# Hybrid pooling and HGRN2 decoder trunk: rectangles of the recurrence from packed key blocks, and the first weights behind the first rows

## The chip, the cores and the metric

One Trainium2 chip, one of its cores. The metric is the device time of one execution in microseconds (us). Three executions of the kernel before took 1765.79 to 1770.45 us, with a median of 1767.56.

## The reference

The input is 1024 tokens of 1024 channels, with 16 learned tokens put in front. There are two layers, each with a residual add: a pooling mixer, then a gated linear recurrence (HGRN2) of 16 heads of 128. All is float32.

```python
def _hgrn_chunk_step(S, xs):
    """One chunk of S_t = diag(f_t) S_{t-1} + k_t i_t^T, o_t = S_t^T q_t."""
    q, k, v, g = xs
    causal = jnp.tril(jnp.ones((c, c), dtype=bool))
    bcum = jnp.cumsum(g, axis=2)
    rel = bcum[:, :, :, None, :] - bcum[:, :, None, :, :]
    decay = jnp.exp(jnp.where(causal[:, :, None], rel, -jnp.inf))
    scores = jnp.einsum('bhtk,bhsk,bhtsk->bhts', q, k, decay)
    o = jnp.einsum('bhts,bhsv->bhtv', scores, v) + jnp.einsum('bhtk,bhkv->bhtv', q * jnp.exp(bcum), S)
    ...
def reference(x, meta_tokens, norm_w, ...):
    h = jnp.concatenate([meta, x], axis=1)
    for i in range(DEPTH):
        hn = rmsnorm(h, norm_w[i])
        y = pool_mixer(hn, ...) if i % N_MIXERS == 0 else hgrn2_mixer(hn, ...)
        h = h + y
    return rmsnorm(h[:, N_META:], final_norm_w)
```

The two big input projections are `h @ w_in` in both mixers; in the recurrence `w_in` gives q, f, i and gate.

## The kernel before

**Products.** The 1040 tokens are two passes of 520, each two halves of 260. A pair of blocks of a projection is made by seven products per pair of weight columns (`products`, names P1, P2, P6, P5, P7, P3, P4), each of 12 matmuls a pass (L413 to L415): the high and low part of the tokens (Th, Tl) with the high and low part of a weight (w). Both parts are made by ACT (a cast, L148) and DVE (a subtraction, L149). A product of both passes is 24 matmuls.

**Order of the work.** After each product `tick` moves a clock on by one and runs what is due. The pieces of a head's recurrence are put on that clock by `later` with the numbers of the table `PIECES`, so they lie between the products of the next head: `to32` at 8, `l32` at 9, `l64` at 10, `turn_k` at 11. Weights are made up to three products ahead (`LOOK`, `fill`). The framework that builds the program may still move an instruction on its engine's queue; each engine runs its own queue in order.

**The recurrence.** A head has Q and K as 128 channels by 1024 tokens, eight chunks of 128 tokens. `score` makes the part of the masked score matrix A inside blocks of 32 tokens from 4 products of a chunk each, 128 columns (L711). `to32` then scales Q and K by the decay of blocks of 32 (L716, L717). A level of block size h (`rect`, called by `level` for `l32` and `l64`) gives the rectangles of A where an odd block of h queries meets the even block of keys ahead of it:

```python
for c in range(NT):
    pe.matmul(b[:, c], lhsT=K0[:, c * P : (c + 1) * P], rhs=q4[:, c, 1::2], start=True, stop=True)
```

There are eight products (L664), one for a chunk, each with all 128 keys of the chunk as weights and its 64 odd queries as columns; half of what comes out isn't used. ACT copies the used blocks to A (L667), and `advance` scales odd Q and even K by the next decay (L655, L656) for the next level. `turn_k` transposes K for the states. A product of float32 operands stands in the profile as two records.

**Buffers.** A pool of 38 SBUF tiles of 128x1040 (`unit`) holds the tokens' parts, Q, K, F and what a head needs for a while.

**The start.** `load_tokens` loads the rows of the first pass in five tiles (16, 128, 128, 128 and 120 rows; `ht`). `first(i)` squares and sums a tile (L348 on ACT), makes rstd (L105 on DVE, L106 on POOL) and scales the rows (L353); `second(i)`, two steps behind, transposes them on PE (L366) and puts them into hn (L371 on ACT, L374 on DVE). `make_T` then builds the T tiles of the seven products from hn (L288). `ensure` loads the raw weights; for the first two raw buffers a copy of rstd is written into the buffer first (L185), so their loads can't be issued ahead of the tile that rstd is of:

```python
if i == 1:
    stat[0] = r
```

Of the kernel before, what the change touches and what calls it, by code (L numbers as in the profile page):

```python
# [14 lines left out]
P = 128  # L15
# [26 lines left out]
    "run": 0, "turn_v": 1, "inv0": 1, "inv1": 2, "scale_q": 2, "inv2": 3, "inv3": 4, "scale_k": 5, "scale_e": 6,  # L42
    "score0": 6, "score1": 7, "to32": 8, "l32": 9, "l64": 10, "turn_k": 11, "states": 12, "outs": 14, "normed": 16, "gated": 17,
}
# [7 lines left out]
def kernel(  # L52
# [38 lines left out]
    def atbank():  # L91
        return ps_at.tile([P, 512], F32, tag="at", name="at")
# [62 lines left out]
    def whole(fast):  # L155
# [171 lines left out]
        def tokens(p, w, ys=None, hts=None, lag=2):  # L327
# [3 lines left out]
            def first(i):  # L331
# [17 lines left out]
                rstd_into(r, ssq, tn, 1, D)  # L349
                if i == 1:  # L350
                    stat[0] = r
# [235 lines left out]
        def mixer1(steps):  # L587
# [61 lines left out]
            def advance(Q, K, h, fcur, fnext):  # L649

                nq, nk = Q.shape[1] // (2 * h), K.shape[1] // (2 * h)
                qe, qo = blocks(Q, h)
                ke, ko = blocks(K, h)
                fe, fo = blocks(fcur, 1)
                vec.tensor_tensor(qo, qo, fe[:, fe.shape[1] - nq :].broadcast_to([P, nq, h]), mul)  # L655
                vec.tensor_tensor(ke, ke, fo[:, fo.shape[1] - nk :].broadcast_to([P, nk, h]), mul)  # L656
                vec.tensor_tensor(fnext, fe[:, :, 0], fo[:, :, 0], mul)

            def rect(Q, K0, h):

                b = atbank().rearrange("p (c i) -> p c i", i=64)
                q4 = Q.rearrange("p (c b i) -> p c b i", c=NT, i=h)
                for c in range(NT):
                    pe.matmul(b[:, c], lhsT=K0[:, c * P : (c + 1) * P], rhs=q4[:, c, 1::2], start=True, stop=True)  # L664
                A3 = A.rearrange("p (c t) -> p c t", t=P)
                for i, s0 in enumerate(range(0, P, 2 * h)):
                    act.copy(A3[s0 : s0 + h, :, s0 + h : s0 + 2 * h], b[s0 : s0 + h, :, i * h : (i + 1) * h])  # L667

            def level(Q, K0, h, fcur, fnext):
                rect(Q, K0, h)  # L670
                advance(Q, K0, h, fcur, fnext)

            def intra_fast(Q, K, F, Fe):
# [40 lines left out]
                def to32():  # L714
                    q32, k32 = (a.rearrange("p (b i) -> p b i", i=32) for a in (Q, K0))
                    vec.tensor_tensor(q32, q32, ee.broadcast_to([P, 32, 32]), mul)  # L716
                    vec.tensor_tensor(k32, k32, eo.broadcast_to([P, 32, 32]), mul)  # L717
                    vec.tensor_tensor(Fe[:, 24:56], ee[:, :, 0], eo[:, :, 0], mul)
# [51 lines left out]
            def scan(n, Q, K, F, ti):  # L770
# [6 lines left out]
                def turn_v():  # L777
                    V = tl["V"] = unit("V")[:, :SEQ].rearrange("p (c v) -> p c v", v=P)
                    Vm = tl["Vm"] = cst.tile([P, P], F32, tag="Vm", name="Vm", bufs=2)
                    for b0 in (0, 4, 8):  # L780
# [5 lines left out]
                        if b0 < 8:  # L786
                            act.copy(V[:, b0 : b0 + 4], b)
                        else:
                            pool.memset(Vm, 0.0)
                            act.copy(Vm[:META], b[:META, 0])  # L790

                def turn_k():
# [60 lines left out]
                def gated():  # L853
# [14 lines left out]
                    "turn_v": turn_v, "turn_k": turn_k, "states": states, "outs": outs, "normed": normed, "gated": gated,  # L868
                    "l32": lambda: level(Q, K0, 32, Fe[:, 24:56], Fe[:, 0:16]),
                    "l64": lambda: level(Q, K0, 64, Fe[:, 0:16], dec),  # L870
                }
# [146 lines left out]
        for i, fn in enumerate(tokens(0, nw[0], hts=hts[0])):  # L1018
            fn()
            if i == 1:  # L1020
                ensure(1)
                hts.append([load_tokens(1, i) for i in range(len(TP[1]))])
            if i == len(TP[0]):
                fill()
# [59 lines left out]
```

## Time and profile before

| | us |
|---|---|
| median of three runs (lowest, highest) | 1767.56 (1765.79, 1770.45) |
| the profiled execution, its own time | 1768.34 |
| its span | 1766.6 |
| PE busy | 1696.1 |
| DVE busy | 1239.5 |
| ACT busy | 786.3 |

The span is what the profiler saw of the core's work; the execution's own time has the little around it too. Busy times are of instructions: PE's matmuls are pipelined, so the records overlap, and what a group of them takes on PE is read from the chain of work or from where the next ones start, not from their durations. An engine that is idle costs time only where the chain passes through its wait.

### The profile page before, as it was taken

Reading aid. Unit: us, or ns where it says so; the run is one execution under the profiler, and the core shown is the slowest. Engines: PE = TensorE matmul, PEld = TensorE weight load, DVE = VectorE, ACT = ScalarE, POOL = GpSimd, SP = SyncE. Lnnn points to the kernel's source line nnn. Section 1 sums busy time; section 2 is a strip of 40 time slices with the busy share of each in tenths; the row PEclk is TensorE's granted clock in tenths of the full one; section 3 lists DMA queues with packets and bytes.
Section 4 is the critical chain, followed back from the end, with each engine's and each line's share of the span. In section 5 each row is a group of like instructions: output and inputs, shape, how many; then the busy total and the mean of one; then the engine's idle time right before and its main releaser. Section 6 shows DMA issues by size and latency. Waiting matters only on the chain.

```text
span 1766.6 us, 32378 instructions
## 1 busy us (share of the span) xinstructions
PE 1696.1 (96%) x13315; PEld 1647.8 (93%) x13315; DVE 1239.5 (70%) x1959; ACT 786.3 (45%) x1746; POOL 55.2 (3%) x102
## 2 busy tenths in 40 slices
PE   3899999999998998799999999999999999999997
PEld 3799999999998998699999999999999999988886
DVE  5866677788237725898887787887887887884332
ACT  4533333345236525645554554544555545554221
POOL 1100000000000000000000000000000000000000
PEclk9799999999999999899999999999999999999999
DMA  4133233358337333222222212222212212254330
GB/s 133 37 127 102 97 97 109 109 188 282 96 113 261 104 112 115 66 77 69 79 62 66 84 61 72 67 65 75 84 49 78 67 61 85 76 175 143 113 107 33
DMA packets 191426, 176.56 MB, mean 100 GB/s; under 512 B 7093, under 2 KB 164485, under 8 KB 191269
## 3 DMA queue, kind: packets, MB, share of 16 engines
q1 hardware_dynamic: 191269, 174.40, 31.0%
q8 instruction: 107, 1.75, 0.4%
q14 instruction: 50, 0.41, 0.1%
HBM read 132.55 MB, written 41.81 MB: 99 GB/s over the span
## 4 chain that ended last, share of the span: by engine, by line
PE 88%; DVE 6%; ACT 2%; DMA 2%; issue 1%; SPq 0%; POOL 0%; DVEq 0%; POOLq 0%; ACTq 0%
PE mm L413 17%; PE mm L415 17%; PE mm L414 17%; PE mm L535 5%; PE mm L536 5%; PE mm L537 5%; PE mm L959 3%; PE mm L960 3%; PE mm L961 3%; PE at L664 3%; PE at L711 2%; PE at L838 2%; PE at L839 2%; PE at L817 1%; DMA ht<-in_x_dram 1%
## 5 line engine op out<-in xcount | busy, mean ns | idle before, releaser
L413 PE MATMUL mm<-Th,w 128*128 128x260 f32 x2688 | 778.9, 290 | 16.7 <-ACT Th L148 5.8
L415 PE MATMUL mm<-Th,w 128*128 128x260 f32 x2688 | 766.3, 285 | 3.1 <-DVE w L149 3.0
L414 PE MATMUL mm<-Tl,w 128*128 128x260 f32 x2688 | 764.5, 284 | 3.3 <-DVE Tl L149 3.2
L413 PEld LDWEIGHTS mm<-Th,w 128*128 128x128 f32 x2688 | 511.2, 190 | 21.4 <-ACT Th L148 8.9
L414 PEld LDWEIGHTS mm<-Tl,w 128*128 128x128 f32 x2688 | 511.7, 190 | 4.3 <-DVE Tl L149 4.3
L415 PEld LDWEIGHTS mm<-Th,w 128*128 128x128 f32 x2688 | 510.9, 190 | 4.4 <-DVE w L149 4.1
L149 DVE TENSOR_TENSOR w<-raw,w 128x512 fp32r<-128x512 f32 x346 | 232.5, 687 | 175.5 <-ACT w L148 161.3
L148 ACT CAST w<-raw 128x512 fp32r<-128x512 f32 x346 | 209.8, 620 | 165.0 <-PE mm L537 107.6
L535 PE MATMUL mm<-a,w 128*128 128x260 f32 x512 | 144.8, 283 | 0.0
L536 PE MATMUL mm<-a,w 128*128 128x260 f32 x512 | 144.3, 282 | 0.0
L537 PE MATMUL mm<-a,w 128*128 128x260 f32 x512 | 143.9, 281 | 0.0
L419 ACT COPY P<-mm 128x520 f32<-128x520 f32 (+1 forms) x153 | 85.8, 561 | 119.0 <-PE mm L415 119.0
L148 ACT CAST w<-S 128x512 fp32r<-128x512 f32 x100 | 60.3, 621 | 128.9 <-DVE S L245 61.5
L692 DVE RECIPROCAL F<-X 128x260 f32<-128x260 f32 x64 | 111.3, 1758 | 0.0
L959 PE MATMUL mm<-woh,w 128*128 128x512 f32 x256 | 101.4, 396 | 0.0
L960 PE MATMUL mm<-wol,w 128*128 128x512 f32 x256 | 100.8, 394 | 0.0
L961 PE MATMUL mm<-woh,w 128*128 128x512 f32 x256 | 100.4, 392 | 0.0
L537 PEld LDWEIGHTS mm<-a,w 128*128 128x128 f32 x512 | 96.3, 188 | 0.0
L536 PEld LDWEIGHTS mm<-a,w 128*128 128x128 f32 x512 | 96.3, 188 | 0.0
L535 PEld LDWEIGHTS mm<-a,w 128*128 128x128 f32 x512 | 96.1, 188 | 0.0
L106 POOL TENSOR_TENSOR rstd<-rstd,nhalf 128x1 f32<-128x1 f32 (+4 forms) x44 | 43.8, 996 | 1112.0 <-DVE rstd L105 1107.6
L535 PE MATMUL mm<-u,w 128*128 128x260 f32 x256 | 74.1, 289 | 4.6 <-DVE hn L374 3.0
(153 smaller groups left out, 2535.1 us busy)
## 6 DMA issues: line engine op xcount, KB each, us to landing
raw<-in_hgrn_w_in_dram SPq DMA_DIRECT2D x68, 512.0 KB, 4.3
raw<-in_pool_w_in_dram SPq DMA_DIRECT2D x32, 512.0 KB, 5.3
raw<-in_pool_w_out_dram SPq DMA_DIRECT2D x32, 512.0 KB, 4.0
u_dram<-d SPq DMA_DIRECT2D x16, 520.0 KB, 2.7
ur<-u_dram SPq DMA_DIRECT2D x32, 260.0 KB, 5.2
sgh<-s_dram SPq DMA_DIRECT2D x32, 260.0 KB, 4.5
raw<-in_pool_w_grp_dram SPq DMA_DIRECT2D x16, 512.0 KB, 4.0
gl<-g_dram SPq DMA_DIRECT2D x32, 256.0 KB, 5.6
```

Source lines behind the costliest of these rows:

```text
L148: act.copy(hi, src)
L149: vec.tensor_tensor(lo, src, hi.bitcast(F32), sub)
L413: pe.matmul(o, lhsT=w[:, 0, ks], rhs=th[:, k], start=first, stop=False, **kw)
L414: pe.matmul(o, lhsT=w[:, 0, ks], rhs=tl[:, k], start=False, stop=False, **kw)
L415: pe.matmul(o, lhsT=w[:, 1, ks], rhs=th[:, k], start=False, stop=k == 3, **kw)
L535: pe.matmul(o, lhsT=w[:, 0, ks], rhs=xs[k][:, 0, cs], start=first and k == 0, stop=False)
L536: pe.matmul(o, lhsT=w[:, 0, ks], rhs=xs[k][:, 1, cs], start=False, stop=False)
L537: pe.matmul(o, lhsT=w[:, 1, ks], rhs=xs[k][:, 0, cs], start=False, stop=last and k == 3)
L692: vec.reciprocal(iX[:, s], X[:, s])
L959: pe.matmul(ps[i][nh], lhsT=w[:, 0, ts], rhs=wh[:, s], start=n == 0, stop=False)
L960: pe.matmul(ps[i][nh], lhsT=w[:, 0, ts], rhs=wl[:, s], start=False, stop=False)
L961: pe.matmul(ps[i][nh], lhsT=w[:, 1, ts], rhs=wh[:, s], start=False, stop=n == HEADS - 1)
```

## The change

In the recurrence a new piece `e32` (at 8, behind `to32`) copies the even blocks of K for h = 32 into a new tile KE, on ACT; `l32` does the same for h = 64 at its end. `rect` then takes 128 columns of KE, the even keys of two chunks side by side, as weights and the 128 odd queries of these two chunks as columns: 4 products a level. The used blocks now lie on the diagonal of what comes out, so there are 4 copies to A for h = 32 and 2 for h = 64, each of half the chunks. In `advance` and `to32` K is scaled ahead of Q.

At the start the raw weights' loads wait for the rstd of the fourth row tile in place of the second, and the loads of the second pass's rows are written behind them there.

```diff
@@
-    "score0": 6, "score1": 7, "to32": 8, "l32": 9, "l64": 10, ...
+    "score0": 6, "score1": 7, "to32": 8, "e32": 8, "l32": 9, "l64": 10, ...
@@
                 rstd_into(r, ssq, tn, 1, D)
-                if i == 1:
+                if i == 3:
                     stat[0] = r
@@
+                vec.tensor_tensor(ke, ke, fo[:, fo.shape[1] - nk :].broadcast_to([P, nk, h]), mul)
                 vec.tensor_tensor(qo, qo, fe[:, fe.shape[1] - nq :].broadcast_to([P, nq, h]), mul)
-                vec.tensor_tensor(ke, ke, fo[:, fo.shape[1] - nk :].broadcast_to([P, nk, h]), mul)
@@
-            def rect(Q, K0, h):
-                b = atbank().rearrange("p (c i) -> p c i", i=64)
-                q4 = Q.rearrange("p (c b i) -> p c b i", c=NT, i=h)
-                for c in range(NT):
-                    pe.matmul(b[:, c], lhsT=K0[:, c * P : (c + 1) * P], rhs=q4[:, c, 1::2], start=True, stop=True)
-                A3 = A.rearrange("p (c t) -> p c t", t=P)
-                for i, s0 in enumerate(range(0, P, 2 * h)):
-                    act.copy(A3[s0 : s0 + h, :, s0 + h : s0 + 2 * h], b[s0 : s0 + h, :, i * h : (i + 1) * h])
+            def rect(Q, ke, h):
+                b = atbank().rearrange("p (c i) -> p c i", i=P)
+                q2 = Q.rearrange("p (c b two i) -> p c b two i", c=NT // 2, two=2, i=h)
+                for c in range(NT // 2):
+                    pe.matmul(b[:, c], lhsT=ke[:, c * P : (c + 1) * P], rhs=q2[:, c, :, 1], start=True, stop=True)
+                A4 = A.rearrange("p (c d t) -> p c d t", d=2, t=P)
+                for j in range(P // h):
+                    d, s0 = divmod(2 * j * h, P)
+                    js = slice(j * h, (j + 1) * h)
+                    act.copy(A4[s0 : s0 + h, :, d, s0 + h : s0 + 2 * h], b[js, :, js])
+
+            def evens(K0, h, ke):
+                act.copy(ke.rearrange("p (b i) -> p b i", i=h), blocks(K0, h)[0])
@@
                 def to32():
+                    vec.tensor_tensor(k32, k32, eo.broadcast_to([P, 32, 32]), mul)
                     vec.tensor_tensor(q32, q32, ee.broadcast_to([P, 32, 32]), mul)
-                    vec.tensor_tensor(k32, k32, eo.broadcast_to([P, 32, 32]), mul)
@@
+                def e32():
+                    tl["KE"] = unit("KE")[:, :SEQ].rearrange("p (h t) -> p h t", h=2)
+                    evens(K0, 32, tl["KE"][:, 0])
+                def l32():
+                    rect(Q, tl["KE"][:, 0], 32)
+                    advance(Q, K0, 32, Fe[:, 24:56], Fe[:, 0:16])
+                    evens(K0, 64, tl["KE"][:, 1])
+                def l64():
+                    rect(Q, tl["KE"][:, 1], 64)
+                    advance(Q, K0, 64, Fe[:, 0:16], dec)
@@
         for i, fn in enumerate(tokens(0, nw[0], hts=hts[0])):
             fn()
-            if i == 1:
+            if i == 3:
                 ensure(1)
                 hts.append([load_tokens(1, i) for i in range(len(TP[1]))])
```

The built programs show where this lands on the engines' queues. ACT's queue of the kernel before, in a steady head around `l32` and `l64` (P is the first product kept, w a weight's high part, KT the transposed keys; K and F of L620 and L621 are the next head's):

```order
L148 CAST w<-raw 128x512 x3
L620 ACTIVATE K<-F 128x2x260
L621 ACTIVATE F<-F 128x2x260
L419 COPY P_9337<-mm 128x520
L148 CAST w<-raw 128x512
L667 COPY A<-at 32x8x32 x2
L419 COPY P_9381<-mm 128x520
L148 CAST w<-raw 128x512
L667 COPY A<-at 64x8x64
```

The same place on ACT's queue in the changed kernel (KE<-K at L673 are the copies of the even blocks, for 32 and then for 64):

```order
L148 CAST w<-raw 128x512 x3
L620 ACTIVATE K<-F 128x2x260
L673 COPY KE<-K 128x512
L621 ACTIVATE F<-F 128x2x260
L419 COPY P_9337<-mm 128x520
L148 CAST w<-raw 128x512
L670 COPY A<-at 32x4x32 x4
L673 COPY KE<-K 128x512
L419 COPY P_9380<-mm 128x520
L148 CAST w<-raw 128x512
L670 COPY A<-at 64x4x64 x2
```

The first KE copy stands behind L620 and the second behind the four copies of `l32`; on PE's queue the products of both levels keep their places.

DVE's queue of the kernel before at the start, from the copies of rstd into the raw buffers on (S are sums of weight blocks):

```order
L185 COPY raw<-rstd 8x1 x2
L244 TENSOR_TENSOR S_270<-raw 128x512
L245 TENSOR_TENSOR S_271<-S_270,raw 128x512
L254 TENSOR_TENSOR raw<-raw 128x512
L149 TENSOR_TENSOR w<-S_271,w 128x512
L105 TENSOR_SCALAR rstd<-ssq 128x1
L353 TENSOR_SCALAR sq<-ht,rstd 128x1024
L374 TENSOR_TENSOR hn<-mm,vecs 128x2x16 x3
L374 TENSOR_TENSOR hn<-mm,vecs 128x2x128 x3
L105 TENSOR_SCALAR rstd<-ssq 128x1
L149 TENSOR_TENSOR w<-S_270,w 128x512
L353 TENSOR_SCALAR sq<-ht,rstd 128x1024
```

The same queue of the changed kernel, from the third tile's rstd on:

```order
L105 TENSOR_SCALAR rstd<-ssq 128x1
L353 TENSOR_SCALAR sq<-ht,rstd 128x1024
L374 TENSOR_TENSOR hn<-mm,vecs 128x2x16 x3
L105 TENSOR_SCALAR rstd<-ssq 128x1
L353 TENSOR_SCALAR sq<-ht,rstd 128x1024
L374 TENSOR_TENSOR hn<-mm,vecs 128x2x128 x3
L185 COPY raw<-rstd 8x1 x2
L374 TENSOR_TENSOR hn<-mm,vecs 128x2x128 x6
L244 TENSOR_TENSOR S_270<-raw 128x512
L245 TENSOR_TENSOR S_271<-S_270,raw 128x512
L105 TENSOR_SCALAR rstd<-ssq 120x1
L254 TENSOR_TENSOR raw<-raw 128x512
```

The third and fourth row tiles and their entries into hn now stand ahead of the first weights' sums. On SP's queue three row tiles of the second pass (8, 128 and 128 rows) stand ahead of the two raw loads where two (8 and 128) did, and two behind them where three did.

## Rows read from the trace of the kernel before

**Rows 1.** The page, busy time, share and instructions of each engine.
```profile
PE 1696.1 (96%) x13315; PEld 1647.8 (93%) x13315; DVE 1239.5 (70%) x1959; ACT 786.3 (45%) x1746; POOL 55.2 (3%) x102
```
**Rows 2.** The page, chain that ended last, by engine.
```profile
PE 88%; DVE 6%; ACT 2%; DMA 2%; issue 1%; SPq 0%; POOL 0%; DVEq 0%; POOLq 0%; ACTq 0%
```
**Rows 3.** Window of one head: us; busy PE, PEld, DVE, ACT, POOL; clock, DMA, GB/s.
```profile
840.00:894.00 54.00, 54.00 (x461) 53.97 (x460) 44.28 (x69) 27.43 (x67) 2.06 (x3) 1.00 0.22 69
```
**Rows 4.** Chain in order of time, 786 to 900 us: start, us, what.
```profile
830.67 0.89 PE at L711 x8
...
841.12 1.73 PE at L664 x16
...
894.91 1.73 PE at L664 x16
```
**Rows 5.** Timeline of DVE at a head's `to32`: start, us, what.
```profile
893.08 0.68 DVE L618 TENSOR_TENSOR F<-P,mm 128x520 f32<-128x520 f32 x1
```
**Rows 6.** Timeline of ACT in the same head, and in the fourteenth.
```profile
893.79 0.64 ACT L620 ACTIVATE K<-F 128x520 f32<-128x520 f32 x1 [1.11 <-DVE F L618]
894.46 0.64 ACT L621 ACTIVATE F<-F 128x520 f32<-128x520 f32 x1
895.01 0.57 ACT L419 COPY P<-mm 128x520 f32<-128x520 f32 x1
...
1539.53 0.64 ACT L620 ACTIVATE K<-F 128x520 f32<-128x520 f32 x1 [1.12 <-DVE F L618]
```
**Rows 7.** Timeline of PE's weight loads at `l32` of the same two heads.
```profile
894.63 1.87 PEld L664 LDWEIGHTS at<-Q,K 128*128 128x128 f32 x16
...
1540.36 1.76 PEld L664 LDWEIGHTS at<-Q,K 128*128 128x128 f32 x15
```
**Rows 8.** Groups of ACT by shape: count, busy us, mean ns, idle before.
```profile
L148 ACT CAST w<-raw 128x512 fp32r<-128x512 f32 x346 | 209.8, 620 | 165.0 <-PE mm L537 107.6 <-PE mm L415 26.4 <-DVE raw L254 18.8
...
L667 ACT COPY A<-at 32x256 f32<-32x256 f32 x32 | 11.6, 363 | 13.5 <-PE at L664 13.2
...
L688 ACT COPY en<-X 128x65 f32<-128x65 f32 x16 | 4.9, 309 | 12.3 <-DVE X L687 12.3
```
**Rows 9.** Timeline of DVE at the start; in brackets idle before and what ended it.
```profile
13.49 0.19 DVE L185 COPY raw<-rstd 8x1 f32<-8x1 f32 x2
21.36 0.69 DVE L244 TENSOR_TENSOR S<-raw 128x512 f32<-128x512 f32 x1 [7.67 <-DMA raw<-in_pool_w_in_dram]
...
24.52 0.15 DVE L105 TENSOR_SCALAR rstd<-ssq 128x1 f32<-128x1 f32 x1 [0.36 <-ACT sq L348]
25.34 0.75 DVE L353 TENSOR_SCALAR sq<-ht,rstd 128x1024 f32<-128x1024 f32 x1 [0.67 <-POOL rstd L106]
26.01 1.37 DVE L374 TENSOR_TENSOR hn<-mm,vecs 128x32 f32<-128x32 f32 x6
...
28.48 0.75 DVE L353 TENSOR_SCALAR sq<-ht,rstd 128x1024 f32<-128x1024 f32 x1 [0.44 <-POOL rstd L106]
...
32.01 1.09 DVE L374 TENSOR_TENSOR hn<-mm,vecs 128x256 f32<-128x256 f32 x3
...
37.00 1.30 DVE L288 TENSOR_TENSOR T<-hn 128x520 f32<-128x520 f32 x2
```
**Rows 10.** Timeline of ACT at the start.
```profile
22.82 0.62 ACT L148 CAST w<-S 128x512 fp32r<-128x512 f32 x1 [10.85 <-DVE S L245]
```
**Rows 11.** Timeline of SP's queue at the start: DMA issues.
```profile
13.66 1.02 SPq L187 DMA_DIRECT2D raw<-in_pool_w_in_dram  x2
```
**Rows 12.** Chain in order of time, at the start.
```profile
7.14 3.66 DMA ht<-in_x_dram
```
**Rows 13.** Windows of the start, columns as in rows 3.
```profile
21.00:25.00 4.00, 0.00 (x0) 0.00 (x0) 2.83 (x5) 2.18 (x7) 0.25 (x1) 1.00 1.03 379
...
40.00:55.00 15.00, 10.34 (x50) 8.83 (x51) 13.16 (x25) 10.78 (x19) 1.64 (x3) 0.66 0.26 71
...
80.00:90.00 10.00, 10.00 (x86) 10.00 (x85) 9.80 (x18) 2.86 (x6) 0.00 (x0) 1.00 0.13 53
```

More of the change, by code (lines that the diff above doesn't have):

```diff
@@ L42 @@
     "run": 0, "turn_v": 1, "inv0": 1, "inv1": 2, "scale_q": 2, "inv2": 3, "inv3": 4, "scale_k": 5, "scale_e": 6,
-    "score0": 6, "score1": 7, "to32": 8, "l32": 9, "l64": 10, "turn_k": 11, "states": 12, "outs": 14, "normed": 16, "gated": 17,
+    "score0": 6, "score1": 7, "to32": 8, "e32": 8, "l32": 9, "l64": 10, "turn_k": 11, "states": 12, "outs": 14, "normed": 16, "gated": 17,
 }
@@ L654, in advance @@
                 fe, fo = blocks(fcur, 1)
+                vec.tensor_tensor(ke, ke, fo[:, fo.shape[1] - nk :].broadcast_to([P, nk, h]), mul)
                 vec.tensor_tensor(qo, qo, fe[:, fe.shape[1] - nq :].broadcast_to([P, nq, h]), mul)
-                vec.tensor_tensor(ke, ke, fo[:, fo.shape[1] - nk :].broadcast_to([P, nk, h]), mul)
                 vec.tensor_tensor(fnext, fe[:, :, 0], fo[:, :, 0], mul)
-            def rect(Q, K0, h):
-                b = atbank().rearrange("p (c i) -> p c i", i=64)
-                q4 = Q.rearrange("p (c b i) -> p c b i", c=NT, i=h)
-                for c in range(NT):
-                    pe.matmul(b[:, c], lhsT=K0[:, c * P : (c + 1) * P], rhs=q4[:, c, 1::2], start=True, stop=True)
-                A3 = A.rearrange("p (c t) -> p c t", t=P)
-                for i, s0 in enumerate(range(0, P, 2 * h)):
-                    act.copy(A3[s0 : s0 + h, :, s0 + h : s0 + 2 * h], b[s0 : s0 + h, :, i * h : (i + 1) * h])
-            def level(Q, K0, h, fcur, fnext):
-                rect(Q, K0, h)
-                advance(Q, K0, h, fcur, fnext)
+            def rect(Q, ke, h):
[10 more added lines that the diff above has]
+                act.copy(ke.rearrange("p (b i) -> p b i", i=h), blocks(K0, h)[0])
             def intra_fast(Q, K, F, Fe):
@@ L868, in scan @@
                     "turn_v": turn_v, "turn_k": turn_k, "states": states, "outs": outs, "normed": normed, "gated": gated,
-                    "l32": lambda: level(Q, K0, 32, Fe[:, 24:56], Fe[:, 0:16]),
-                    "l64": lambda: level(Q, K0, 64, Fe[:, 0:16], dec),
+                    "e32": e32, "l32": l32, "l64": l64,
                 }
```

## The prediction

> **What bounds the kernel now.** I read the busy shares first: TensorE (PE) is busy for 96% of the span [rows 1]. The chain that ended last is PE for 88% [rows 2]. Both are averages, so I next read PE by stage. In the recurrence (the sixteen heads, 787 to about 1600 us) a window of 54 us shows PE busy throughout, at full clock, with VectorE (DVE) at 44 us and ScalarE (ACT) at 27 [rows 3]. The chain in order of time shows one head's l32 at 841.12 and the next head's at 894.91, so a head is 53.8 us [rows 4]. In such a stage whatever PE no longer does comes off the end, as long as no new wait takes its place. The start is different: there PE waits for the first rows and weights, and only from 80 us is it busy throughout [rows 13].
>
> A change of under 0.3% (5.3 us) can't be told from none with this kernel. The sum is made against the profiled execution, 1768.3 us (span 1766.6), which stands 0.8 above the median of 1767.6.
>
> **PE's part of the rectangles.** A level now has 4 products of 128 columns for 8 of 64. A product is two passes in the records. Eight products of 64 columns, 16 passes, hold the chain for 1.73 us, or 0.108 a pass; four score products of 128 columns, of the same kind and operands, 8 passes, hold it for 0.89, or 0.111 [rows 4]. So the columns hardly count, the number of passes does, and a level falls from 1.73 to 0.89. There are 2 levels in 16 heads: 32 x 0.84 = **26.9 us less**. I take it whole, as all of it lies on PE in a stage where PE has no idle time [rows 3]. The bound from below, nothing, is a rival below.
> The Trainium skill, "TensorE: Matmul & The Clock Gate", section "Back-to-back issue gap", has a rule that speaks against the change: an isolated product's gap is its columns over 2.4 GHz plus 2.5 ns. By it 128 columns would take nearly twice what 64 take, and the 26.9 us would be near 0. The rows just named disagree with it for products that each load new weights.
>
> **ACT's new work, and the wait it makes.** A head gets two copies of 128x512 between SBUF tiles (KE). The nearest row is the cast of 128x512 from SBUF, 0.62 us [rows 8]. The copies out of the PSUM bank get smaller and more: 32x256 takes 0.36 [rows 8] and the copy of P with 520 columns 0.57 [rows 6], so a copy is about 0.16 plus 0.8 ns a column; 4 of 128 columns for 2 of 256 and 2 of 256 for one of 512 are then some 0.3 and 0.15 more. Together 1.7 us a head on an engine that has 26 to spare: by itself nothing. DVE does the same operations in another order.
>
> What counts is when KE is there. Before, PE's l32 waited for DVE alone, which is through with to32 when it starts F at 893.08 [rows 5]. Now it waits for ACT too, and in 13 of the 16 heads the built order puts the KE copy on ACT behind the sigmoid that writes K of the *next* head (L620), which waits for F from DVE (L618). I follow one head. Nothing ahead of this on DVE moves: to32's two products only change places, so F still starts at 893.08 and ends at 893.76 [rows 5]; L620 runs from 893.79 to 894.43 [rows 6]. The KE copy starts between 894.34 (ACT's next instruction may start 0.09 before an end, as the copy of P at 895.01 does after L621) and 894.46 (where L621 starts now) [rows 6]. With 0.62 it ends at 894.96 to 895.08. Handing over takes 0.03 (DVE's end at 893.76, L620's start). So PE can load l32's first weights at about 895.0 to 895.1; today it does so at 894.63 [rows 7]. PE stands still for 0.37 to 0.48 us; I take 0.4. The same order holds in a 14th head, and all fourteen stand alike in time: in the last of them L620 ends at 1540.17 [rows 6] and l32's weights load at 1540.36 [rows 7], as 894.43 and 894.63 here. In head 0 and the last head the orders differ, and I count no wait: **14 x 0.4 = 5.6 us given back**. Bounds: nothing, if the copy were done in 0.2; and, if it ran at the pace of the strided copy of 65 columns, 0.31 us or, less the 0.16, 2.3 ns a column [rows 8], it would take 1.3 us and the wait would be 1.1, in all 15.4.
>
> Behind the KE copy ACT holds L621, the copy of P, a weight cast, the four copies of A and the second KE copy, for l64. With the delay L621 ends at 895.7, P's copy at 896.1, the cast at 896.7, four copies of 0.27 at 897.7, and KE for l64 at 898.3. DVE has K ready for it at 896.9, as K's factor now goes ahead of Q's and no longer waits for PE. PE comes to l64 at 895.1 + 0.9 for l32 + 2.9 for a product = 898.9. So there the cover is 0.6 us, and l64 costs nothing; without that cover every 0.1 us late costs 1.4 us over the heads. P's copy and the cast are 0.5 late, and the weights are made three ticks of 2.9 us ahead. KE takes one buffer more of the shared units for three ticks; the built order shows no wait for a release in a steady head: nothing.
>
> **The start.** DVE copies rstd into the raw buffers at 13.49, which lets SP issue the first weights at 13.66, and then stands until they land at 21.36, 7.67 us [rows 9, 11]. ACT has a cast of DVE's sums of these weights in front of the square of the third row tile; it waits 10.85 us, to 22.82 [rows 10], although the rows were issued from 7.14 and the first tile of 128 landed 3.66 us later [rows 12]. Now the third and fourth tile go ahead of the weights on ACT and DVE. Their two scalings (0.75 each), two rstd (0.15 each) and 12 products into hn (1.37 for six and 1.09 for each three more) fill 5.4 us of DVE's empty time, and its waits of 0.36 for ACT and of 0.67 and 0.44 for POOL lie under the wait for the weights [rows 9]: 6.9 us gained.
> Against it, the weights come later. The row tiles land one behind the other from 7.14 + 3.66 on, some 1.4 us apart (512 KB at 379 GB/s, the rate of a full queue [rows 13]), so the fourth's square can start at some 13.7; its rstd, scaling and the hn of the second tile end at 18.5, and the weights are issued at 18.6 instead of 13.66. On a free queue 512 KB takes 3.66 [rows 12] and the next 1.4 more, so both are there at 23.9 instead of 21.36: 2.5 us lost. That leaves **4.4 us**. The first T, at 37.00 [rows 9], comes to about 32, as one weight's subtraction (0.65) also moves behind it. Up to 80 us DVE is the chain with PE waiting on it [rows 13], so the lead should last until PE is full. Bounds: 2 us, if the two row tiles issued behind the weights take 2.8 us of the queue from them; 6.9, if the weights came as early as now.
>
> **Sum.** 1768.3 - 26.9 + 5.6 - 4.4 = 1742.6; in terms of the median 0.8 less, **1742 us**.
>
> **The rivals.**
> *The copy is hidden.* ACT reaches KE before PE needs it and l32 never waits: 1736. For it: to32's K is done 1.2 us earlier than now. Against: L620 stands in front on ACT in 14 heads. Chance 0.15.
> *Both levels wait.* The strided copy takes 1.3 us: l32 waits 1.1, and the second KE, 0.7 longer itself and behind a queue 0.7 later, ends 0.3 or more after PE comes to l64. 14 x 1.4 = 20 us instead of 5.6: 1756. Against: the copies of A in blocks of 32 show no such pace [rows 8]. Chance 0.09.
> *The start gives nothing:* 1746, the later weights taking all. Chance 0.1, and it lies in the range.
> *Columns set PE's pace:* 8 passes of 0.216 are the 1.73 of today, the copies still make PE wait: 1768.3 + 5.6 - 4.4, or 1769. The 0.111 of the scores speaks against it [rows 4]. Chance 0.03.
> *Slower: PE's clock falls in the new gap.* Between 40 and 55 us, where PE stood still between products, the granted clock averages 0.66, that is 1.2 GHz for much of it [rows 13]; 15 x 0.34 = 5.1 us of full-clock work are missing there. One such fall behind l32 in each of the 14 heads would cost 71 us: 1813. It turns the sign from 6 heads on (25.7 / 5.1 = 5.04). Against: the gap is 0.4 us in 52, while from 40 to 55 PE was busy for only 10.3 us of 15. Chance 0.03.
>
> **How the numbers follow.** The forecast has 0.6. Taking the best bounds (no wait, start 6.9) gives 1734, the worst (15.4, start 2) 1754; so the range is **1734 to 1754**; outside it lie most of both levels waiting, the columns and the clock, 0.13 in all, and a little for what no row shows. The first three rivals are all faster than 1762.3, as is the forecast: faster 0.94. Columns and half-made gains: same 0.03. The clock: slower 0.03.
>
> **What would show it.** L665 (the new product) with 256 records in place of 512, and 0.89 us a level in the chain; a head of 52.5 us; PE idle 0.3 to 0.5 us ahead of l32 in heads 1 to 14, ended by ACT's KE copy, and none ahead of l64; KE copies of about 0.62; the first T at 32 and PE full from some 75 us. It is wrong if a head lasts over 53 us, if PE waits at l64, if the granted clock falls after 90 us, or if the first T comes after 35.

## The result, and the profile after

The changed kernel takes 1740.15 us (median of 4 executions, 1739.94 to 1741.19); the kernel before, run beside it, 1766.96 (1765.79 to 1770.45). The ratio is 0.9841, with a 95% interval of 0.9828 to 0.9854. The profiled execution took 1740.35 us with a span of 1738.5: 28.0 or 28.1 less than in the one of before. The forecast was 1742.0, with a range of 1734 to 1754.

PE and the chain, from the page of the kernel after, answer to [rows 1, 2]:

```profile
PE 1670.9 (96%) x13059; PEld 1620.7 (93%) x13059; DVE 1238.4 (71%) x1959; ACT 809.0 (47%) x1826; POOL 55.4 (3%) x102
...
PE 87%; DVE 6%; DMA 3%; ACT 2%; issue 2%; POOL 0%; SPq 0%; POOLq 0%; DVEq 0%; ACTq 0%
```

PE has 256 instructions less, ACT 80 more. The groups of instructions by shape show which (count, busy us, mean ns of one, idle time ahead and what ended it; L665 is the new product, L673 the copy of the even blocks, L670 the copies to A):

```profile
L665 PE MATMUL at<-Q,KE 128*128 128x128 f32 x256 | 35.2, 280 | 0.0
L665 PEld LDWEIGHTS at<-Q,KE 128*128 128x128 f32 x256 | 31.3, 191 | 2.6 <-ACT KE L673 2.4
L673 ACT COPY KE<-K 128x512 f32<-128x512 f32 x32 | 19.6, 613 | 2.0 <-DVE K L718 0.8 <-DVE K L655 0.8
L670 ACT COPY A<-at 32x128 f32<-32x128 f32 x64 | 16.3, 255 | 1.2 <-PE at L665 0.2
L670 ACT COPY A<-at 64x256 f32<-64x256 f32 x32 | 11.7, 366 | 2.1 <-PE at L665 1.8
```

The chain in order of time, over a head, answers to [rows 4] (start, us, what):

```profile
836.17 1.12 PE at L665 x8
840.05 0.89 PE at L665 x8
877.91 0.89 PE at L713 x8
881.70 0.89 PE at L713 x8
888.48 1.11 PE at L665 x8
892.36 0.89 PE at L665 x8
```

A level is now as long as four score products (L713), 0.89 us, and a head (836.17 to 888.48) is 52.3 us long where it was 53.8. The first level, l32, has 0.22 us more in the chain: a wait. ACT's timeline at this level shows what for, beside [rows 6]:

```profile
887.23 0.64 ACT L620 ACTIVATE K<-F 128x520 f32<-128x520 f32 x1 [1.10 <-DVE F L618]
887.78 0.60 ACT L673 COPY KE<-K 128x512 f32<-128x512 f32 x1
888.29 0.63 ACT L621 ACTIVATE F<-F 128x520 f32<-128x520 f32 x1
...
890.93 0.62 ACT L673 COPY KE<-K 128x512 f32<-128x512 f32 x1
```

And PE's weight loads there, beside [rows 7]:

```profile
887.95 0.19 PEld L415 LDWEIGHTS mm<-Th,w 128*128 128x128 f32 x1
888.08 0.19 PEld L413 LDWEIGHTS mm<-Th,w 128*128 128x128 f32 x1
888.43 0.97 PEld L665 LDWEIGHTS at<-Q,KE 128*128 128x128 f32 x8 [0.17 <-ACT KE L673]
889.32 0.19 PEld L414 LDWEIGHTS mm<-Tl,w 128*128 128x128 f32 x1
...
892.08 0.98 PEld L665 LDWEIGHTS at<-Q,KE 128*128 128x128 f32 x8
```

The KE copy starts 0.09 before L620 ends, ends at 888.38, and PE loads 0.05 later. Loads otherwise follow each other in 0.12; here it is 0.35, so 0.23 is lost (0.24 on average). The waits of PE's weight loads, over the whole trace, count 14 of these (us in total, times, the longest; the 2.4 leave out the time that a load takes to be issued):

```profile
PEld at L665 <- ACT KE L673: 2.4, 14, 0.2
```

The copy for l64 ends at 891.55, 0.53 before PE comes.

At the start DVE's timeline (beside [rows 9]) has the weights' wait cut to 4.11 us, and the first T at 32.72 where it was at 37.00:

```profile
24.34 0.69 DVE L244 TENSOR_TENSOR S<-raw 128x512 f32<-128x512 f32 x1 [4.11 <-DMA raw<-in_pool_w_in_dram]
...
32.72 1.30 DVE L288 TENSOR_TENSOR T<-hn 128x520 f32<-128x520 f32 x2
```

The windows of [rows 3, 13], in the kernel after (columns as there):

```profile
840.00:894.00 54.00, 54.00 (x458) 53.79 (x457) 45.39 (x71) 30.18 (x75) 2.26 (x4) 1.00 0.26 80
21.00:25.00 4.00, 0.00 (x0) 0.00 (x0) 0.66 (x1) 1.14 (x2) 0.00 (x0) 0.50 1.12 347
...
40.00:55.00 15.00, 11.18 (x50) 9.78 (x49) 11.21 (x23) 10.81 (x21) 2.52 (x4) 0.50 0.25 72
...
80.00:90.00 10.00, 10.00 (x86) 10.00 (x85) 9.16 (x17) 3.44 (x8) 0.00 (x0) 1.00 0.20 80
```

A head is full at full clock, as before. The start isn't: PE's granted clock is 0.50 (1.2 GHz) from 40 to 55 us where it was 0.66. From 21 to 25 the column has 0.50 where it had 1.00, but that 1.00 is no full clock. The column takes off recorded stretches at half alone, and ahead of a trace's first one PE's own pace shows half: in all fourteen traces the row transposes at 14 us follow each other in 0.21 us (0.11 at full clock), with 1.00 in the column. In the kernel before, whose first recorded stretch begins at 41.9, products follow each other in 0.22 us up to 38.3 and in 0.12 from 38.5:

```profile
37.85 0.42 PE L414 MATMUL mm<-Tl,w 128*128 128x260 f32 x1
38.07 0.42 PE L415 MATMUL mm<-Th,w 128*128 128x260 f32 x1
...
38.49 0.29 PE L414 MATMUL mm<-Tl,w 128*128 128x260 f32 x1
38.62 0.28 PE L415 MATMUL mm<-Th,w 128*128 128x260 f32 x1
```

So up to a trace's first recorded fall the clock is read from this pace; behind it the column and the pace agree.

To see what is left of the start, I count the weight loads of the products (L413 to L415; 12 a product and pass) and compare when the same load comes in both kernels:

| load | 0 | 12 | 36 | 48 | 72 | 84 | 180 |
|---|---|---|---|---|---|---|---|
| before, us | 32.52 | 37.42 | 46.63 | 50.66 | 56.58 | 61.63 | 82.89 |
| after, us | 29.19 | 32.42 | 42.35 | 46.94 | 55.45 | 60.76 | 81.91 |
| lead | 3.3 | 5.0 | 4.3 | 3.7 | 1.1 | 0.9 | 1.0 |

The lead of 4.3 us that T brings is there, and most of it is gone between the 48th and the 72nd load (two products, P7 and P3, which lie next to the second pass's first row transposes).

### The profile page after: what moved, and what is told of

It is laid out like the page before. It is cut to its first block, busy times and chain, and to the rows that moved or that the text cites. A ratio compares the mean times of both kernels' runs of the same rounds, so it can differ in the third digit from the quotient of the medians.

```text
span 1738.5 us, 31997 instructions
## 1 busy us (share of the span) xinstructions
PE 1670.9 (96%) x13059; PEld 1620.7 (93%) x13059; DVE 1238.4 (71%) x1959; ACT 809.0 (47%) x1826; POOL 55.4 (3%) x102
## 4 chain that ended last, share of the span: by engine, by line
PE 87%; DVE 6%; DMA 3%; ACT 2%; issue 2%; POOL 0%; SPq 0%; POOLq 0%; DVEq 0%; ACTq 0%
PE mm L413 17%; PE mm L415 17%; PE mm L414 17%; PE mm L535 5%; PE mm L536 5%; PE mm L537 5%; PE mm L975 3%; PE mm L973 3%; PE mm L974 3%; PE at L665 2%; PE at L713 2%; PE at L853 2%; PE at L854 2%; DMA ht<-in_x_dram 1%; PE at L832 1%
## 5 line engine op out<-in xcount | busy, mean ns | idle before, releaser
L413 PE MATMUL mm<-Th,w 128*128 128x260 f32 x2688 | 778.5, 290 | 16.3 <-ACT Th L148 6.6
L415 PE MATMUL mm<-Th,w 128*128 128x260 f32 x2688 | 767.5, 286 | 2.5 <-DVE w L149 2.2
L413 PEld LDWEIGHTS mm<-Th,w 128*128 128x128 f32 x2688 | 511.7, 190 | 20.9 <-ACT Th L148 7.9
L415 PEld LDWEIGHTS mm<-Th,w 128*128 128x128 f32 x2688 | 511.6, 190 | 4.0 <-DVE w L149 3.6
```

Of the source, the lines that this page charges most:

```text
L413: pe.matmul(o, lhsT=w[:, 0, ks], rhs=th[:, k], start=first, stop=False, **kw)
L415: pe.matmul(o, lhsT=w[:, 1, ks], rhs=th[:, k], start=False, stop=k == 3, **kw)
```

## The experiments

Theories. **For the heads:** the saving goes by passes (rival: by columns), and the wait at l32 is due to the KE copy standing behind L620. **For the start:** theory A, the half clock of 21 to 55 us eats the lead; theory B, the lead goes to the pace at which DVE and ACT make T and weights, and the clock is a side effect. In the table: the median of each kernel and its ratio to the kernel before on the same chip; of the profiled execution the span, the time lost ahead of l32 (worked out as above), the mean head from the second to the fifteenth l32, the time from the 48th to the 72nd load and how much of it had the half clock, and the 180th load.

| | median | ratio (95%) | span | wait l32 | head | 48th to 72nd (half) | 180th |
|---|---|---|---|---|---|---|---|
| before | 1766.96 | 1 | 1766.6 | 0 | 53.81 | 5.92 (1.5) | 82.89 |
| after | 1740.15 | 0.9841 (0.9828, 0.9854) | 1738.5 | 0.24 | 52.30 | 8.51 (8.0) | 81.91 |
| start alone | 1767.17 | 0.9991 (0.9982, 1.0) | 1765.3 | 0 | 53.85 | 8.94 (8.9) | 82.12 |
| rectangles alone | 1742.08 | 0.9847 (0.9833, 0.9861) | 1739.7 | 0.24 | 52.25 | 5.99 (1.8) | 83.08 |
| early K32 | 1739.94 | 0.9832 (0.9818, 0.9845) | 1738.9 | 0 | 52.08 | 8.94 (8.9) | 82.05 |
| 64 columns | 1743.48 | 0.9851 (0.9836, 0.9866) | 1741.9 | 0.24 | 52.30 | 8.56 (8.1) | 82.04 |
| extra products, 1 | 1741.61 | 0.985 (0.9831, 0.9868) | 1739.4 | 0.24 | 52.30 | 8.52 (8.0) | 84.19 |
| the same, i == 1 | 1744.43 | 0.9862 (0.9845, 0.988) | 1747.8 | 0.24 | 52.25 | 7.77 (6.5) | 84.98 |
| the same, early K32 | 1739.79 | 0.9845 (0.9826, 0.9863) | 1738.1 | 0 | 52.08 | 8.94 (8.9) | 81.98 |
| extra products, 2 | 1741.95 | 0.9835 (0.981, 0.986) | 1739.7 | 0.24 | 52.30 | 8.02 (6.0) | 81.02 |
| the same, early K32 | 1736.85 | 0.9814 (0.9791, 0.9837) | 1735.6 | 0 | 52.08 | 6.85 (3.4) | 81.42 |
| i == 2 | 1742.6 | 0.9846 (0.9822, 0.987) | 1740.3 | 0.24 | 52.30 | 6.12 (2.0) | 81.08 |
| i == 2, early K32 | 1739.78 | 0.9837 (0.9821, 0.9853) | 1736.6 | 0 | 52.06 | 6.04 (1.8) | 81.38 |
| early K32 again | 1739.67 | 0.9835 (0.9819, 0.9852) | 1737.9 | 0 | 52.08 | 8.52 (8.0) | 81.72 |

### The start alone

The kernel before with the two lines of the start.

```diff
-                if i == 1:
+                if i == 3:
                     stat[0] = r
...
-            if i == 1:
+            if i == 3:
                 ensure(1)
```

> The kernel before with the start's change alone (the first weights wait for the fourth row tile). Theory A: the lead that the start wins is lost again in the first products, as PE runs them at half clock for longer; PE's 180th product matmul comes about 1 us earlier than before, and the time falls by 1 us (1766 for a before of 1767). Rival B: the lead of 3.4 us that the changed kernel shows when the recurrence begins is the start's, and the time falls by 3.4 (1763.6). Rival C: the 4.4 of the prediction lasts (1762.6).

Measured: 0.9991 (0.9982 to 1.0), that is 0 to 3.2 us less. The 48th load comes 3.0 us ahead of before, the 72nd not at all (56.62 against 56.58), the 180th 0.8. So the start is worth about 1 us at the point from which PE is full, not 4.4, and its loss lies in the same two products as in the kernel after.

### The rectangles alone

The kernel after with the old start.

```diff
-                if i == 3:
+                if i == 1:
                     stat[0] = r
...
-            if i == 3:
+            if i == 1:
                 ensure(1)
```

> The changed kernel with the start of before: the rectangles' change alone. Theory A: 32 levels fall from 1.79 to 0.90 us (28.5 saved) and 14 heads wait 0.24 us at l32 (3.4 given back), 25.1 us less than before, 1742 for a before of 1767. Rival B, with 3.4 us due to the start: 23.4 less, 1743.6. Both: a steady head of 52.3 us.

Measured: 0.9847, a head of 52.25 us, and no lead at the 180th load (83.08). The rectangles carry the result: 26.8 us by the medians, of 26.8 in the kernel after.

### K's 32-blocks scaled and copied a step earlier

If the wait is due to the KE copy's place behind L620, it must go when the copy gets another place. Here `to32` is cut in two: K's half and the copy are due at 7, behind `score1`, which reads no K0 after that.

```diff
-    ... "score1": 7, "to32": 8, "e32": 8, "l32": 9, ...
+    ... "score1": 7, "k32": 7, "e32": 7, "to32": 8, "l32": 9, ...
...
+                def k32():
+                    k = K0.rearrange("p (b i) -> p b i", i=32)
+                    vec.tensor_tensor(k, k, eo.broadcast_to([P, 32, 32]), mul)
                 def to32():
...
-                    vec.tensor_tensor(k32, k32, eo.broadcast_to([P, 32, 32]), mul)
```

> The changed kernel with K's scaling by blocks of 32 and the first KE copy one tick earlier, behind score1, so that on ACT the copy stands ahead of the next head's sigmoid (L620). Theory A (the 0.24 us at l32 is ACT's order, not the copy's length): no wait at l32, a head of 52.0 us in place of 52.3, 14 x 0.24 = 3.4 us less than the changed kernel, 1736.8. Rival: the wait only moves (the weight cast behind the copy, or F's start, comes late): a head of 52.3 us or more, 1740 or slower.

Measured: no wait for KE at l32 in any head; the chain in order of time now has both levels alike:

```profile
891.47 0.89 PE at L665 x8
895.25 0.89 PE at L665 x8
```

A head takes 52.08 us, 0.22 less, and the stretch from the second to the fifteenth l32 2.8 less than in the kernel after. The edit moves K's scaling on DVE too, but that was not what came late: in the kernel after it ends at 885.46, 2.3 us ahead of the start of the copy at 887.78.

```profile
884.24 1.22 DVE L718 TENSOR_TENSOR K<-K,en 128x1024 f32<-128x1024 f32 x1
```

So it was the copy's place on ACT that made the wait. But the time hardly moves: 1739.94, and 1739.67 when run again, ratios 0.9832 and 0.9835 where the kernel after has 0.9841, with intervals that overlap. Part of what the heads gave is given back in the first head, which takes 53.4 us where it took 52.5: by the waits of PE's weight loads in that head, the transposed K (`turn_k`, L822 here) is late once, for the products of the states (waited for; us in total, times, longest):

```profile
PEld at L833 <- ACT KT L822: 1.2, 1, 1.2
```

The kernel after has no such wait. That leaves some 2 us, and single executions differ by as much. Run again, the same kernel has this wait twice, 2.2 us in all, the second time in the last head.

### Half the columns

The same four weight loads, but 64 columns instead of 128; the second chunk's rectangles are copied from the first's.

```diff
-                    pe.matmul(b[:, c], lhsT=ke[...], rhs=q2[:, c, :, 1], start=True, stop=True)
+                    pe.matmul(b[:, c, :64], lhsT=ke[...], rhs=q2[:, c, : 64 // h, 1], start=True, stop=True)
...
-                    act.copy(A4[...], b[js, :, js])
+                    cs = slice(j * h % 64, j * h % 64 + h)
+                    act.copy(A4[...], b[js, :, cs])
```

> The changed kernel with 64 columns in place of 128 in each of the 4 products of a level; the second chunk's rectangles are then copied from the first's. Theory A (a pass costs its weight load, whatever the columns): 256 passes get 0.003 us shorter each, under 1 us in all, 1739.3. Rival (columns set the pace): a level falls from 0.90 to 0.47 us, 32 x 0.43 = 14 us less, 1726.

Measured: a head of 52.30 us, as with 128 columns, and the chain of a level without a wait:

```profile
843.30 0.84 PE at L665 x8
```

The last product's columns are 0.05 shorter at the level's end; from first load to the next product's load it is 0.90 with either width. So the number of passes, each with its own weights, sets a level's time. The rival by columns has fallen. Whether it is the load of the weights or the pass as such isn't told apart: in every run a pass has one load.

### Extra products to keep the clock up

These test theories A and B at the start: the kernel after with products whose result nobody reads, put where PE has nothing to do. The first set has 44 transposing products behind the row transposes, and 10, 20, 12 and 6 products of 260 columns behind the parts of P1, P2, P6 and P5 (the trace has the last 18 of them together, ahead of P5).

```diff
+                    if ys is None and p == 0 and i - lag == 3:
+                        warm(44)
...
+                if passes == (0,) and kept is not None and {'P1': 10, 'P2': 20, 'P6': 12, 'P5': 6}.get(name):
+                    bw = atbank()
+                    for _ in range({'P1': 10, 'P2': 20, 'P6': 12, 'P5': 6}[name]):
+                        pe.matmul(bw[:, :CH], lhsT=w[:, 0, :P], rhs=T[name][0][1][:, 3], start=True, stop=True)
```

> The kernel after, with 92 extra products whose result nobody reads, all in the first 55 us: 44 transposing products of 128x128 behind the row transposes of the 4th tile (where TensorE of the kernel after idles from 18.4 to 27.8 us), and 10, 20, 12 and 6 products of 128x260 behind the first part of P1, P2, P6 and P5 (where it idles for 1.3 to 2.4 us each). The order on VectorE, ScalarE and the queues stays as it was. Theory A (the half clock of 20.8 to 34.5 and 37.9 to 55.0 us ate the start's lead): with TensorE kept busy the clock is granted in full there, a product takes 0.11 in place of 0.215 us, and the 180th weight load of the products (81.9 us in the kernel after) comes 2 to 3 us earlier, by 79 to 80; the time falls by as much, to about 1737.5. Theory B (the lead was lost to the pace at which VectorE and ScalarE make the first T and weights, the clock is a side effect): the clock rises, but the 180th load stays at 81.5 to 82.2 and the time at 1740 +- 1. If the extra products stand in the way of real ones, both are later.

Measured: by PE's pace the clock is at half up to 23.0 us, in the midst of the 44, then full to 47.0, then at half until 57.3. The 44 were two passes each, 11.2 us in all, and held up the last row transposes, so the first products come 3.3 us later. Two stretches tell the theories apart: from the 12th to the 36th load, and from the 48th to the 72nd. In the kernel before, in windows of PE alone (window, us, PE busy with its count, granted clock, DMA share, GB/s; the first 0.74 counts the half clock up to 38.4 us as full):

```profile
37.42:46.63 9.21, 5.34 (x27) 0.74 0.00 0
...
50.66:56.58 5.92, 5.45 (x40) 0.88 0.09 24
```

In the kernel after:

```profile
32.42:42.35 9.93, 5.60 (x26) 0.67 0.00 0
...
46.94:55.45 8.51, 8.04 (x40) 0.53 0.42 120
```

With the extra products:

```profile
35.11:44.63 9.52, 8.02 (x66) 1.00 0.01 2
...
49.21:57.73 8.52, 8.05 (x39) 0.53 0.42 119
```

From the 12th to the 36th load the clock hardly matters: 9.52 us at full clock, 9.93 at 0.67. PE is idle there for some 4 us, waiting for T; theory B holds for this stretch. From the 48th to the 72nd PE is idle for 0.47 us in all three, and the rest is its own work, at half clock in two of them and mostly at full clock in the kernel before. There the theories are not yet apart, since the clock fell at 47 us in spite of the extra products.

The same set without the 44, on the rectangles alone:

> Rectangles alone (first weights loaded behind the second row tile, as before), with the same 10, 20, 12 and 6 extra products behind the parts of P1, P2, P6 and P5; the 44 ahead of them are left out, since rows arrive later here. Without the extra products its 180th load is at 83.1 us and the clock is at half from 42 to 53 us. Theory A: the clock stays full there, the 180th load comes about 1 us earlier, at 82, and the time is about 1741; the difference to the same with the first weights behind all rows is 2 to 3 us. Theory B: 83 and 1742, and the difference stays about 1 us.

Neither theory's numbers came. The half clock didn't go, it moved, from 42.3 to 52.5 us into 36.9 to 40.3 and 50.5 to 57.4, and with it the stretch went from 5.99 us to

```profile
50.92:58.69 7.77, 7.30 (x40) 0.59 0.08 21
```

and the 180th load from 83.08 to 84.98. The 48th came at 50.92, against 50.76 without the extra products; the extra ones all lie ahead of it, and the order on DVE and ACT is the same. So the same work behind the same start takes 1.8 us longer with 4.7 us more of half clock in it.

The first set with the early K32:

> The kernel after with the key side scaled for 32-row blocks and its even blocks copied one step earlier (as in the run in which the wait at the first level was gone), and with the 92 extra products. The two effects lie in different stages and should add: by theory A about 1736.5 to 1738, by theory B about 1739 to 1740. No wait at either level, a head takes 52.1.

Again half from 46.5 us on, 8.94 in the stretch, and 1739.79: nothing over the early K32 alone.

The second set has 22 in place of the 44, 18 behind P6, and 10 more ahead of P5 that go to free columns of P7's bank and alter that bank's sums.

> The kernel after with extra products as in the first run of this kind, but the row stage gets 22 (each of those turned out to be two passes, and 44 of them held the last row transposes up by 4 us) and the gap ahead of P5 28 in place of 18. There the clock fell to half at 47.0 us, as P7 began, so the stretch from the 48th to the 72nd weight load (P7 and P3) still ran at half and took 8.5 us, as in the kernel after, where the kernel before takes 5.9. Theory A' (up to the 48th load the making of T sets the pace and the clock costs nothing; from there to the 72nd TensorE does, and half a clock costs the 2.6 us that the lead loses there): if the clock now stays full past 47 us, that stretch takes 6 to 7 us and the 180th load comes at 79.5 to 80.5 (81.9 in the kernel after), the time 1738; if the clock falls at 47 all the same, the stretch takes 8.5 and the 180th load comes at 81.9. Theory B (the clock is a side effect): 8.5 us with a full clock too.

> The same extra products in the kernel whose key side is scaled and copied one step earlier. What the clock does between 40 and 57 us decides as in the run before; heads take 52.1 without a wait. Theory A' with a full clock: 1737; with half a clock from 47 us, or theory B: 1739 to 1740.

Now, after earlier falls, the clock fell at 49.0 us in the first of these and at 50.7 in the second, and the stretch is 8.02 and

```profile
48.10:54.95 6.85, 6.12 (x40) 0.75 0.53 150
```

The 180th load comes at 81.02 and 81.42. The second of them has the lowest median of all, 1736.85, 3 us below the early K32 alone, but on another chip and with intervals that overlap. By the spans it is 3.3, and 2.7 of these lie between the 180th load and the first l32, where its trace has 13.7 us of half clock for 17.1; so I don't read them as the start's.

### The first weights behind the third row tile

The kernel after with i == 2 for i == 3 in the two lines of the start.

> The kernel after with the first weights loaded behind the third row tile instead of behind the fourth (i == 2 for i == 3). Its order on TensorE is like that with i == 1. Both theories: the first products lie between those of i == 1 (32.6 us) and i == 3 (29.2 us). Theory A': the lead is worth at most 1 us at the 180th load (81.9 to 83.1), and which part of it is left goes by how much of the stretch from the 48th to the 72nd load lies in half a clock: 6 us with little of it, 8.5 us with all of it. Time 1739 to 1742.

Here the half clock ends at 50.7 us, early in the stretch:

```profile
48.64:54.76 6.12, 5.65 (x40) 0.83 0.02 4
```

The 180th load comes at 81.08, 0.8 ahead of the kernel after, although the 48th comes 1.7 behind it. The median, 1742.6 (1739.54 to 1744.94), doesn't show it.

The fourteen traces together settle the stretch. In the order of the half clock in it, 1.5, 1.8, 1.8, 2.0, 3.4, 6.0, 6.5, 8.0 (three), 8.1 and 8.9 us (three), it takes 5.92, 5.99, 6.04, 6.12, 6.85, 8.02, 7.77, 8.51 to 8.52, 8.56 and 8.94: 0.41 us more for each us of half clock ((8.94 - 5.92) / (8.9 - 1.5)), whatever the start, the levels or the extra products; the traces between these ends lie up to 0.25 us off. The DMA share, which differs too in these windows, does not order them: 7.77 us came with 0.08 and 6.85 with 0.53.

### Both together

The early K32 with i == 2, and the early K32 once more beside it on the same chip.

> Both parts in the form that the runs so far favour: the key side scaled and copied one step earlier (no wait at the first level, a head 52.1 us) and the first weights loaded behind the third row tile (the stretch from the 48th to the 72nd weight load 6.1 us, the 180th load at 81.1). Against the kernel after that is 14 x 0.24 = 3.4 us less in the heads and 0.8 us less at the 180th load, so 1736 to 1737 if nothing is given back; the run with the early key side alone, which expected 3.4 and got 0.2, says that single falls of the clock between 550 and 740 us move a run by up to 2 us, so 1736 to 1740. Rival: the start's order with i == 2 falls back into the half clock, 8.5 us in that stretch, 1740.

> The kernel with the early key side once more, unchanged, beside the run above on the same chip: its heads again 52.1 us without a wait, 1739 to 1740. The difference to the run above is then what the start alone is worth: 0 to 1 us by the 180th load (82.0 against 81.1).

Measured: 1739.78 and 1739.67. By the traces the first has 6.04 us in the stretch in place of 8.52 and its 180th load 0.3 earlier; the medians don't tell them apart. Neither beats the kernel after by more than the executions scatter.

## Why the prediction was right

The verdict, the size and the range held, but two terms were off by more than their reasons, in opposite directions. By the profiled pair, 28.1 us of span were saved where the steps add up to 25.7. That these lie so close is in part luck: the heads gave 3.4 us more than their two terms (24.7 for 21.3), the start 3.4 less, and 2.4 came from a stretch in which no term lies. One by one:

**PE's part of the rectangles: 28.5 for 26.9.** The mechanism was as said: passes, not columns, and the saving is whole, since PE has no idle time in a head. The term was sized from the chain, 1.73 to 0.89. From a level's first load to the next product's, before was 1.79 (894.63 [rows 7] to 896.42), and after is 0.90 (888.43 to 889.32): 0.89 for each of 32 levels.
The Trainium skill, "TensorE: Matmul & The Clock Gate", section "Back-to-back issue gap", is not the rule against the change that the prediction takes it for: it gives the gap by columns for an isolated product, and says that in a stream of weight loads and products both set the spacing, so that this gap under-counts at small widths. The run with 64 and the kernel with 128 columns, 0.90 us a level both, agree with that. Its 81 ns a product at 128 columns was not reached: a pass takes 112 (0.90 / 8).

**The wait at l32: 3.4 for 5.6.** It came in the 14 heads and from the instruction that was named, with a copy of 0.60 us where 0.62 were expected and a start 0.09 before L620's end. It was 0.24 instead of 0.4, because the place of l32 on PE's queue was not quite kept, as the text ahead of the prediction had it: one matmul of the next product (the L413 at 888.08) now stands ahead of it, and covers 0.12. Before, l32's first load followed an L415, the last of a product. At 0.37 to 0.48 less 0.12, what came is just under the lower end. That the copy's place behind L620 makes the wait is shown by the run in which it went. l64 waits for nothing, as forecast, with 0.53 to spare for 0.6.

With these two the heads should give 25.1 us; from the first l32 to the end it is 24.7 (979.6 to 954.9).

**The start: 1.0 for 4.4.** This is the step that failed. Its sum was right as far as it went: the weights landed at 24.34 for 23.9 (its own terms, 18.6 + 3.66 + 1.4, give 23.7), the first T came at 32.72 for 32, and the 36th load has a lead of 4.3. What failed is "up to 80 us DVE is the chain with PE waiting on it, so the lead should last until PE is full". [rows 13] are busy times, from which no chain can be read. The chain of the kernel before, in order of time, is DVE from 32.01 to 47.91 and then PE up to 58.95, with 0.39 us of ACT in it:

```profile
46.69 1.18 DVE Tl L149
47.91 0.59 PE mm L414
...
50.66 0.59 PE mm L413
...
58.04 0.89 PE mm L366 x8
58.95 0.63 ACT hn L371 x2
```

DVE and ACT do set the pace up to the 48th load: with a full clock there (the run with i == 1 and extra products) it comes no earlier. Then come 24 matmuls with the row transposes between them in which PE is the bound, and how long they take goes by PE's clock. In the kernel before the half clock of 41.9 to 52.1 fell mostly on the stretch ahead, where PE waits and the clock costs nothing; in the kernel after the earlier start put the stretch into the half clock of 37.9 to 55.0. That took 2.6 of the 3.7 us. The rival "the start gives nothing" was nearer to this than the forecast, but by its price, not by its mechanism: the weights landed 3.0 us later, little more than the 2.5 of the forecast.

What could have told it was on hand: this chain, and the 0.66 of the window from 40 to 55 us [rows 13], which was read only as a danger for the heads. Together they say that the start has work of PE on the chain that takes longer if it lies in the wrong place.

**Between the 180th load and the first l32: 2.4 for nothing.** No term of the change lies there. The profiled execution of before takes 704.1 us for it and that of after 701.7. Over all fourteen, the four with 10 to 14 us of half clock in this time take 700.2 to 701.9, the ten with 17 to 21 us take 701.7 to 707.8, and which is which doesn't follow the edits; before has 17.1 us, after 13.7. The early K32, one kernel run twice, takes 703.7 us with 17.1 and 701.9 with 10.2. So I take the 2.4 for scatter between executions. That it is nothing else isn't shown; without it the saving would be 25.7 us, and the medians say 26.8.

**The rivals.** The hidden copy (1736) and the wait at both levels (1756) didn't come; the first is what the early K32 makes on purpose, and its worth is less than the 5.6 that lay between it and the forecast. Columns as PE's pace is refuted by the run with half of them. The clock didn't fall in the new gap: 1.00 in the window of a head.

**The signs.** Three of those that were named came out otherwise. The wait at l32 is 0.24 us and not 0.3 to 0.5. PE isn't full from 75 us: it is busy for 4.24 of the 5 us from 75 to 80, and was for 4.14 before. And the clock does fall after 90 us, at 696.7, 727.4 and 1730.9, which was to show the prediction wrong. The kernel before has such falls too (570.9, 700.7, 710.9, 731.4 and 1762.2); in both kernels none lies in the heads, so they say nothing against the rectangles.

## What to carry to other kernels

Where each small fp32 product loads its own weights, count loads, not columns (64 and 128 took the same here): packing the used halves of two products into one load halved the time of a level, and one copy on an idle engine pays for it, if that copy isn't put behind an instruction that comes late. A lead at the start is worth only what is left of it where the busiest engine becomes full, so follow it from product to product and look at that engine's clock in each stretch on the way. And a wait that goes is a gain only if the next late thing isn't as late: here K's transposes took a third of it back in the first head (0.9 of 2.8 us).

## What the runs showed of the hardware

- PE's clock in the first 80 us goes between its two levels (2.4 and 1.2 GHz) at places that small edits move. Both kernels begin at half, with 0.21 us a row transpose. In the kernel after, 24 of these come in one go (13.8 to 18.4 us); from 17.4 on they follow each other in 0.11, and after an idle time the clock falls at 20.8, to 34.5, and again from 37.9 to 55.0. In the kernel before, with 8 transposes and a longer idle time behind them, it is still at half when PE works again from 26.15, rises at 38.4, in the midst of the first products, and falls again from 41.9 to 52.1. Why just there, no run here tells.
- The page's granted clock can't be taken for the start: it reads 1.00 ahead of a trace's first recorded fall, where PE's pace is that of half (0.22 us a product up to 38.3 us in the kernel before, 0.12 from 38.5).
- Keeping PE busy moved the late half clock and didn't remove it: with the extra products it fell at 47.0, 50.5, 46.5, 49.0 and 50.7 us. In three of these five runs it also fell earlier, at 36.9, at 28.5, and at 20.0 and 30.3; in the two with 44 products behind the row transposes it was full from about 20 or 23 us up to the late fall.
- In the stretch from the 48th to the 72nd load, 24 matmuls and the transposes between them take some 5.3 us at full clock (5.92 less 1.5 x 0.41) and 8.94 at half, 1.7 times as long and not twice. So some 1.7 us of it don't follow the clock (5.3 - (8.94 - 5.3)), of which 0.47 shows as PE's idle time.
- From 550 to 750 us every trace has single falls of the clock, of 3.4 to 13.6 us each, at places that differ from run to run. PE isn't full around them (6.99 of the 10 us from 730 to 740 in the kernel before). One kernel run twice, the early K32, differs by 1.8 us in the time up to the first l32 (703.7 and 701.9), with 17.1 and 10.2 us of half clock in it, which hides gains of the size of the early K32.
